# adaLN products moved to TensorE strips, low parts moved from GpSimd, and the RG-LRU output norm folded into the projection, in a transformer block on one core

## The chip, the core and the metric

The kernel runs on one core of one Trainium2 chip. The core has TensorE (PE, matrix products; its weight loads are listed as PEld), VectorE (DVE), ScalarE (ACT), GpSimd (POOL), and SyncE (SP), whose queue starts nearly all DMAs. The metric is the device time of one execution in microseconds, the median of several runs; lower is better.

## The reference, cut to what matters

One block of width 1024 over 2048 rows, all in fp32. `c` conditions both norms through a product with a 1024 x 6144 matrix (adaLN):

```
c_act = silu(c)
sh1, sc1, g1, sh2, sc2, g2 = split(c_act @ ada_w + ada_b, 6)
h = rmsnorm(x, mix_norm_g) * (1 + sc1) + sh1
z = h @ w_in                       # 1024 x 2328, split into q, keys, values, gates, zx, zy
o_nsa = three-branch sparse attention(q, keys, values, gates)
o_lru = RG-LRU scan(conv(zx)) * gelu(zy)
mixed = concat(rmsnorm(o_nsa, nsa_out_norm_g), rmsnorm(o_lru, lru_out_norm_g))
x = x + g1 * (mixed @ w_out)
h = rmsnorm(x, ffn_norm_g) * (1 + sc2) + sh2
x = x + g2 * conv_ffn(h)
return rmsnorm(x, final_norm_g)
```

## The kernel before

Every large product is made of fp32r pieces: an operand is split into a high part `h` (a copy rounded to fp32r, by ACT) and a low part `l` (the rest, by a subtraction), and `mm3` sums the three products hh, hl and lh. So each weight tile and each input tile costs an ACT copy and a subtraction before PE can use all of it. The order of the instructions on every engine is set when the program is built, by a scheduler that plays a time line; on the chip each engine takes its own instructions in that order.

The program has three phases. Phase 1 makes the in-projection in four chunks of 512 rows; phase 2 makes the attention and the output projection in 16 tiles of 128 rows; phase 3 makes the feed forward in four chunks.

Phase 1 starts with the modulation of the first norm. `ada_pair(k)` makes the shift and the scale of the features of block k (two blocks of 128 columns of the adaLN matrix, 512 KB each, loaded to `adp`). It does so in one of three ways by the letter in `HOW`: D and M multiply the eight row tiles by `c_act` and add them up on DVE (`aa`, lines 225 and 227; for M half of it on ACT and POOL, lines 230 and 233), and P uses eight products on PE with one column of `c_act` as the weights (`apr`, line 215). A product with ones then sums `aa` over the partitions (`ap`, line 234), and DVE adds the bias (`mod`, line 235). The other 32 blocks of the matrix are made by `ada_block`, one after each in-projection tile (`ada_next`), always on DVE: one multiplication (line 168) and seven multiply-adds (line 170) into `aa`, then a product with ones (`ap`, lines 173 and 182). Their 512 KB inputs `ad` share the five buffers of the tag `x`.

Each chunk needs its rows normalised and transposed. `norm_x` loads four tiles of rows, ACT squares and scales them (lines 140 and 142); `norm_k` then makes one feature block of `hT`: four transposes on PE (`tp`, line 149), `hh` on ACT (line 153), `hf` on DVE (line 154), `hl` on POOL (line 155). Eight such blocks make the chunk's input.

Then PE makes the tiles of the chunk in this order: `zc` (two), `zx` (four, RG-LRU input), `zy` (four, its gate), `zq` (four), `zk` (two), `zv` (four, values and gates); the first four tiles of the first chunk are called `zf`. The weights of a tile are loaded to `wr` (512 KB), and their high and low parts are `w..h` (ACT, line 120) and `w..l` (POOL, line 121), three tiles deep. Between them the RG-LRU runs: convolution `xc` on DVE, its parts `xs`, the gate products `pg`, decay, scan (line 380), and `yy`, whose squares are summed to `sqs` (POOL, line 388). `lru_norm` sums `sqs` over the partitions with one fp32 product of 512 columns (`pr`, line 392), takes the square root and the reciprocal of it (`rb`, lines 394 and 395), multiplies `yy` by it (line 397) and stores high and low parts `ls` (POOL, line 401). In chunks 1 to 3 `wo_next` also scales rows of `w_out` (`wos`, DVE, line 316) from two loads, `g1b` and `wor`.

After the last chunk's value tiles come the compressed keys and values (`ph`, with inputs `xbh` and `xbl`), and phase 2 begins with the first score product `sa`.

Of the kernel before, what the change touches and what calls it, by code (L numbers as in the profile page):

```python
# [50 lines left out]
def hymba_block(ctx, tc, x, vecs, rows, ada, w_in, w_v, lru_w, cmp_w1, cmp_w2, w_out, w_gu, w_dn,  # L51
# [9 lines left out]
    # scratch in DRAM: what one phase hands to the next  # L61
# [10 lines left out]
    # ---------------------------------------------------------------- constants  # L72
# [19 lines left out]
    epsb = cst.tile([P, 1], F32, name="epsb")  # L92
    pool.memset(epsb, EPS)
# [7 lines left out]
    gates = cst.tile([P, NQ, 24], F32, name="gates")  # L101
    VC = cst.tile([P, G, P], F32R, name="VC")
# [14 lines left out]
    def split(pl, raw, shape, name, tag, bufs, lo_eng=None):  # L117
# [28 lines left out]
    def norm_k(pl, pp, xs, c, k, Acol, Bcol, hbufs):  # L146
# [52 lines left out]
    with tc.tile_pool(name="a", bufs=1, reuse_waits="tile") as pl, tc.tile_pool(name="ap", bufs=1, space=PSUM, reuse_waits="tile") as pp:  # L199
# [377 lines left out]
        while adaq:  # L577
            ada_next()
# [462 lines left out]
```

## Time and profile before

| | us |
|---|---|
| median of the three runs | 3023.27 |
| lowest and highest of them | 3020.88, 3027.9 |
| profiled execution: span from its first to its last instruction | 3027.4 |
| TensorE busy in that span | 2853.5 (94%) |
| VectorE, ScalarE, GpSimd busy | 1872.6, 1457.8, 1662.2 |
| phase 1, up to the first score product | about 657 |

The profile gives the profiled execution as its span alone; that is 4.1 us (0.14%) above the median of the runs. All times inside the program are counted from the span's start. A product's busy time runs to its modelled end and overlaps the next one, so the pace of products is read from the distance of their starts.

### The profile page before, as it was taken

The numbers are of one execution on the slowest core, as the hardware profiler recorded it, in microseconds if no ns is written. First come the engines' busy times: TensorE is split into PE (matmuls) and PEld (weight loads), VectorE is DVE, ScalarE is ACT, GpSimd is POOL, SyncE is SP. The second block draws the span as 40 slices with busy tenths as digits, with TensorE's granted clock in tenths as the row PEclk, the third lists the DMA queues.
The fourth block names the chain that finished last, engine by engine and source line by source line (L and its number), as shares of the span: only waits on it lengthen the run. The fifth ranks groups of instructions, "written<-read, shape, count | busy, mean of one in ns | idle before, by whom it ended". The sixth has DMA issues, their size and how long they took to land. (4 is left out here: it accounts for less than half of the span.)

```text
span 3027.4 us, 39397 instructions
## 1 busy us (share of the span) xinstructions
PE 2853.5 (94%) x13676; PEld 2344.7 (77%) x13676; DVE 1872.6 (62%) x3373; ACT 1457.8 (48%) x2619; POOL 1662.2 (55%) x1584
## 2 busy tenths in 40 slices
PE   6989888968999999999999999999999999999998
PEld 4767676756778887888778888788887888888886
DVE  7778888775777888888756650466405663056620
ACT  4636353556677777777743332433325333233322
POOL 4555646557666566555534464644546445464444
PEclk8989899978999999999999999999999999999999
DMA  6465646555444433344253332433324333243332
GB/s 241 151 205 170 221 154 229 158 172 173 134 134 123 121 107 117 107 120 125 74 191 98 96 124 94 140 97 98 128 88 146 98 97 128 82 139 97 96 100 84
DMA packets 233064, 397.84 MB, mean 131 GB/s; under 512 B 20385, under 2 KB 143265, under 8 KB 232609
## 3 DMA queue, kind: packets, MB, share of 16 engines
q1 hardware_dynamic: 232256, 394.13, 41.0%
q8 instruction: 109, 1.79, 0.2%
q0 software_dynamic: 320, 1.05, 0.1%
q14 instruction: 91, 0.74, 0.1%
q10 hardware_dynamic: 288, 0.13, 0.0%
HBM read 342.16 MB, written 53.08 MB: 131 GB/s over the span
## 5 line engine op out<-in xcount | busy, mean ns | idle before, releaser
L906 DVE TENSOR_SCALAR ac<-gp,vec 128x512 f32<-128x512 f32 x88 | 189.2, 2150 | 215.3 <-ACT gp L903 208.2
L750 DVE TENSOR_TENSOR tl<-pt,th 128x512 fp32r<-128x512 f32 (+4 forms) x444 | 295.6, 684 | 40.8 <-ACT th L749 37.2
L749 ACT ACTIVATE th<-pt 128x512 fp32r<-128x512 f32 (+4 forms) x444 | 254.6, 593 | 111.8 <-PE pt L748 106.7
L938 DVE TENSOR_TENSOR o<-pt,o 128x128 f32<-128x128 f32 x128 | 28.3, 283 | 435.8 <-PE pt L935 435.8
L720 POOL TENSOR_SCALAR ps<-ps,rs,gates 128x1024 f32<-128x1024 f32 (+7 forms) x192 | 181.4, 956 | 146.3 <-DVE rs L717 93.1
L914 DVE TENSOR_TENSOR gl<-ac,gh 128x512 fp32r<-128x512 f32 x88 | 212.2, 2411 | 68.9 <-ACT gh L913 68.9
L909 ACT ACTIVATE ac<-ac 128x512 f32<-128x512 f32 x88 | 55.7, 632 | 316.2 <-DVE ac L908 316.2
L714 ACT ACTIVATE ps<-ps,mn 128x1024 f32<-128x1024 f32 (+7 forms) x192 | 171.1, 895 | 35.6 <-DVE mn L614 35.3
L748 PE MATMUL pt<-ident,ps 128*128 128x128 f32 x1088 | 168.4, 275 | 5.3 <-DVE tl L750 4.4
L121 POOL TENSOR_TENSOR wd_0l<-wd,wd_0h 128x1408 fp32r<-128x1408 f32 x32 | 103.1, 3223 | 126.1 <-ACT wd_0h L120 126.1
L609 PE MATMUL ss<-ks,Q 128*128 128x512 f32 (+3 forms) x640 | 165.3, 382 | 4.7 <-DVE mn L614 2.1
L748 PEld LDWEIGHTS pt<-ident,ps 128*128 128x128 f32 x1088 | 134.1, 141 | 41.6 <-DVE tl L750 10.8
L121 POOL TENSOR_TENSOR wd_1l<-wd,wd_1h 128x1408 fp32r<-128x1408 f32 x32 | 103.2, 3224 | 110.6 <-ACT wd_1h L120 110.6
L908 DVE SCALAR_TENSOR_TENSOR ac<-gp,vec,ac 128x512 f32<-128x512 f32 x176 | 137.9, 783 | 6.1
L609 PEld LDWEIGHTS ss<-ks,Q 128*128 128x128 f32 x640 | 117.0, 196 | 31.6 <-DVE mn L614 6.4
L128 PE MATMUL pd<-gl,wd_0h 128*128 128x512 f32 x352 | 139.8, 397 | 0.0
L128 PE MATMUL pd<-gh,wd_0h 128*128 128x512 f32 x352 | 137.7, 391 | 0.0
L128 PE MATMUL pd<-gl,wd_1h 128*128 128x512 f32 x352 | 137.6, 391 | 0.0
L128 PE MATMUL pd<-gh,wd_0l 128*128 128x512 f32 x352 | 137.5, 391 | 0.0
L128 PE MATMUL pd<-gh,wd_1l 128*128 128x512 f32 x352 | 137.5, 390 | 0.0
L128 PE MATMUL pd<-gh,wd_1h 128*128 128x512 f32 x352 | 137.4, 390 | 0.0
L760 PE MATMUL po<-tl,vs 128*128 128x512 f32 x272 | 123.4, 454 | 2.0 <-DVE tl L750 2.0
(1564 smaller groups left out, 9053.4 us busy)
## 6 DMA issues: line engine op xcount, KB each, us to landing
wg<-in_w_gu_dram SPq DMA_DIRECT2D x88, 512.0 KB, 3.5
wu<-in_w_gu_dram SPq DMA_DIRECT2D x88, 512.0 KB, 3.5
wd<-in_w_dn_dram SPq DMA_DIRECT2D x64, 704.0 KB, 4.0
wr<-in_w_in_dram SPq DMA_DIRECT2D x64, 512.0 KB, 4.3
ad<-in_ada_dram SPq DMA_DIRECT2D x32, 512.0 KB, 5.4
Q<-Q_d SPq DMA_DIRECT2D x64, 256.0 KB, 4.0
ks<-K_d SPq DMA_DIRECT2D x56, 256.0 KB, 3.5
vs<-V_d SPq DMA_DIRECT2D x56, 256.0 KB, 3.0
```

The costliest lines, as they stand in the source:

```text
L121: (lo_eng or pool).tensor_tensor(l, raw, h.bitcast(F32), op=OP.subtract)
L128: pe.matmul(ps, a, b, start=(n == 0), stop=(n == total - 1))
L609: pe.matmul(ps[:, o:o + W], Qt[:, hl, h * P:(h + 1) * P], K_ap, start=(hl == 0), stop=(hl == 1))
L714: act.activation(p, p, AF.Exp, scale=-1.0, bias=init, accum_out=sm[:, h, 2 + n:3 + n])
L720: pool.tensor_scalar(p, p, rs[:, h, 2:3], gt[:, h, 1:2], op0=OP.mult, op1=OP.mult)
L748: pe.transpose(pt[:, h * P:(h + 1) * P], jobs[n][0](h), ident)
L749: act.activation(th, pt, AF.Copy)
L750: dve.tensor_tensor(tl, pt, th.bitcast(F32), op=OP.subtract)
L760: pe.matmul(po, jobs[n][1], tl, start=False, stop=(n == N - 1))
L906: dve.tensor_scalar(ac, gp[:, 0:TC], V("fcw", f), V("fcb", f), op0=OP.mult, op1=OP.add)
L908: dve.scalar_tensor_tensor(ac, gp[:, k:k + TC], V("fcw", k * NF + f), ac, op0=OP.mult, op1=OP.add)
L914: dve.tensor_tensor(l, ac, h.bitcast(F32), op=OP.subtract)
```

## The change

1. **adaLN on PE.** `caz` holds `c_act` as eight weight tiles of 32 columns, of which 31 are zero. `ada_product` multiplies a block's eight row tiles by them with eight fp32 products of 128 columns; row tile q writes the 32 partitions from 32 (q mod 4) on, so the first four start four strips of one PSUM tile and the other four add to them. ACT copies the strips to SBUF (`adr`), and a product with ones sums them over the partitions (`ada_columns`, line 179, or line 192 for the gate of the residual), one step later than the product for the 32 later blocks. All eight pairs and all 32 blocks go this way; `aa` and `HOW` are gone. The later blocks load into one buffer of their own (`ad`), and the tag `x` has four buffers instead of five.
2. **Low parts.** In phase 1 `split` subtracts on DVE: weights, `xs`, `ls`. Phase 3's weights stay on POOL (`wload`). `sqs` is summed on DVE.
3. **Norm.** `hl` no longer comes from POOL: DVE makes `hf` as ps * A - hh, and ACT adds the bias and rounds. This holds for phase 1 and for the three later chunks of phase 3.
4. **RG-LRU output norm.** `lru_out` stores `yy` without the norm, and 16 products of one column give the row sums; their inverse root `rlru` is the scale of ACT's copy of the projection's first half in phase 2.

Cut to what the text speaks of, comments aside:

```diff
-        (lo_eng or pool).tensor_tensor(l, raw, h.bitcast(F32), op=OP.subtract)
+        (lo_eng or dve).tensor_tensor(l, raw, h.bitcast(F32), op=OP.subtract)
...
-        dve.tensor_scalar(f, ps, Acol[:, k:k + 1], Bcol[:, k:k + 1], op0=OP.mult, op1=OP.add)
-        pool.tensor_tensor(l, f, h.bitcast(F32), op=OP.subtract)
+        dve.scalar_tensor_tensor(f, ps, Acol[:, k:k + 1], h.bitcast(F32), op0=OP.mult, op1=OP.subtract)
+        act.activation(l, f, AF.Identity, bias=Bcol[:, k:k + 1])
...
+    def ada_product(pl, pp, caz, raws, name):
+        n = len(raws)
+        ps = pp.tile([P, n * P], F32, name=f"apr{name}", tag="g", bufs=2)
+        for j, raw in enumerate(raws):
+            for q in range(KT):
+                o = 32 * (q % 4)
+                pe.matmul(ps[o:o + 32, j * P:(j + 1) * P], caz[:, q, :], raw[:, q, :], start=(q < 4), stop=(q >= 4))
+        r = pl.tile([P, n * P], F32, name=f"adr{name}", tag="adr", bufs=2)
+        act.activation(r, ps, AF.Copy)
+        return r
+    def ada_columns(pp, r, b, n, step, name):
+        p1 = pp.tile([P, n], F32, name=f"ap{name}", tag="g", bufs=2)
+        for j in range(n):
+            pe.matmul(p1[:, j:j + 1], r[:, j * P:(j + 1) * P], ones[:, 0:1], start=True, stop=True)
+        cols = slice(b, b + (n - 1) * step + 1, step)
+        o = VEC["ada_b"][0] + b
+        dve.tensor_tensor(mod[:, cols], p1, vec[:, o:o + (n - 1) * step + 1:step], op=OP.add)
+    def ada_steps(pl, pp, caz, b):
+        raw = pl.tile([P, KT, P], F32, name=f"ad{b}", tag="ad", bufs=1)
         sync.dma_start(raw, ada[b])
-        acc = pl.tile([P, P], F32, name=f"aa{b}", tag="adacc", bufs=2)
-        dve.tensor_scalar(acc, raw[:, 0, :], cact[:, 0:1], None, op0=OP.mult)
-        for k in range(1, KT):
-            dve.scalar_tensor_tensor(acc, raw[:, k, :], cact[:, k:k + 1], acc, op0=OP.mult, op1=OP.add)
+        r = ada_product(pl, pp, caz, [raw], f"b{b}")
...
-            pe.matmul(ps, ones, acc, start=True, stop=True)
+            pe.matmul(ps, ones, r, start=True, stop=True)
...
-            ps = pp.tile([P, 1], F32, name=f"ap{b}", tag="g", bufs=2)
-            pe.matmul(ps, acc, ones[:, 0:1], start=True, stop=True)
-            dve.tensor_tensor(mod[:, b:b + 1], ps, V("ada_b", b), op=OP.add)
+            ada_columns(pp, r, b, 1, 1, f"c{b}")
+        yield
...
-                ("junk", 2048, 1), ("ii", 8192, 1), ("th", 8192, 1), ("yy", 8192, 1), ("x", 4096, 5), ("t2", 2048, 2),
+                ("ii", 8192, 1), ("th", 8192, 1), ("yy", 8192, 1), ("x", 4096, 4), ("ad", 4096, 1), ("t2", 2048, 2),
...
+        caz = pl.tile([P, KT, 32], F32, name="caz")
+        dve.memset(caz, 0.0)
+        dve.tensor_copy(caz[:, :, 0:1], cact.unsqueeze(2))
...
-            if how == 'P':
-                ps = pp.tile([1, 2 * P], F32, name=f"apr{k}", tag="g", bufs=2)
-                for q in range(KT):
-                    pe.matmul(ps, cact[:, q:q + 1], raw[:, :, q, :], start=(q == 0), stop=(q == KT - 1))
-                r = pl.tile([1, 2 * P], F32, name=f"adr{k}", tag="ge", bufs=2)
-                act.activation(r, ps, AF.Copy)
-            for j in range(2):
-                p1 = pp.tile([P, 1], F32, name=f"ap{k}_{j}", tag="g", bufs=2)
-                if how == 'P':
-                    pe.matmul(p1, r[:, j * P:(j + 1) * P], ones[0:1, 0:1], start=True, stop=True)
-                else:
-                    acc = pl.tile([P, P], F32, name=f"aa{k}_{j}", tag="adacc", bufs=2)
-                    if j == 0 or how == 'D':
-                        dve.tensor_scalar(acc, raw[:, j, 0, :], cact[:, 0:1], None, op0=OP.mult)
-                        for q in range(1, KT):
-                            dve.scalar_tensor_tensor(acc, raw[:, j, q, :], cact[:, q:q + 1], acc, op0=OP.mult, op1=OP.add)
-                    else:
-                        for q in range(KT):
-                            act.activation(raw[:, j, q, :], raw[:, j, q, :], AF.Copy, scale=cact[:, q:q + 1])
-                        for w in (4, 2, 1):
-                            dst = raw[:, j, 0:w, :] if w > 1 else acc.unsqueeze(1)
-                            pool.tensor_tensor(dst, raw[:, j, 0:w, :], raw[:, j, w:2 * w, :], op=OP.add)
-                    pe.matmul(p1, acc, ones[:, 0:1], start=True, stop=True)
-                dve.tensor_tensor(mod[:, 8 * j + k:8 * j + k + 1], p1, V("ada_b", 8 * j + k), op=OP.add)
+            r = ada_product(pl, pp, caz, [raw[:, 0], raw[:, 1]], f"p{k}")
+            ada_columns(pp, r, k, 2, 8, f"p{k}")
...
-        ada_pair(0, "xc", HOW[0])
-        xs0 = norm_x(pl, x, 0, 5)
+        ada_pair(0, "xc")
+        xs0 = norm_x(pl, x, 0, 4, ("t2", 2))
...
+        adap = []
         def ada_next():
+            new = None
             if adaq:
-                ada_block(pl, pp, adaq.pop(0), "x", 5)
+                new = ada_steps(pl, pp, caz, adaq.pop(0))
+                next(new)
+            if adap:
+                next(adap.pop())
+            if new:
+                adap.append(new)
 
...
-                    pool.tensor_tensor(sqs, sqs, t2, op=OP.add)
-
-            def lru_norm():
-                pr = pp.tile([P, TC], F32, name=f"pr{c}", tag="g", bufs=2)
-                pe.matmul(pr, ones, sqs, start=True, stop=True)
-                rb = pl.tile([P, TC], F32, name=f"rb{c}", tag="sqs", bufs=1)
-                act.activation(rb, pr, AF.Sqrt, scale=1.0 / 512.0, bias=epsb)
-                dve.reciprocal(rb, rb)
+            def lru_out():
                 for m in range(4):
-                    dve.tensor_tensor(yy[:, m], yy[:, m], rb, op=OP.mult)
                     if c + 1 < NCH:
                         st = pl.tile([P, 2, TC], F32R, name=f"ls{c}_{m}", tag="st", bufs=3)
                         act.activation(st[:, 0], yy[:, m], AF.Copy)
-                        pool.tensor_tensor(st[:, 1], yy[:, m], st[:, 0].bitcast(F32), op=OP.subtract)
+                        dve.tensor_tensor(st[:, 1], yy[:, m], st[:, 0].bitcast(F32), op=OP.subtract)
                         sync.dma_start(L_d[:, :, m, t0:t0 + TC], st.bitcast(F32))
                     else:
                         for n, t in enumerate(split(pl, yy[:, m], [P, TC], f"ls{c}_{m}", "h", 12)):
                             sync.dma_start(L_d[:, n, m, t0:t0 + TC], t.bitcast(F32))
-
-            # --- attention inputs
+                pr = pp.tile([P, 4], F32, name=f"pr{c}", tag="g", bufs=2)
+                for t in range(4):
+                    pe.matmul(pr[:, t:t + 1], sqs[:, t * P:(t + 1) * P], ones[:, 0:1], start=True, stop=True)
+                rl = rlru[:, 4 * c:4 * c + 4]
+                dve.tensor_scalar(rl, pr, 1.0 / 512.0, EPS, op0=OP.mult, op1=OP.add)
+                pool.tensor_tensor(rl, rl, nhalf, op=OP.pow)
...
-                act.activation(t, p1, AF.Copy)
+                act.activation(t, p1, AF.Copy, scale=rlru[:, i:i + 1])
...
-            return split(pl, raw, [P, n, P], name, "w", 2, lo_eng)
+            return split(pl, raw, [P, n, P], name, "w", 2, lo_eng or pool)
```

What moves on TensorE in the first chunk's first key tile (`zk`, 24 products): before, the sum of the adaLN block `aa` stands behind the tile's sixth product.

```order
L128 MATMUL zk_0_1293<-hh_1_225,w14h 128x512
L128 MATMUL zk_0_1293<-hl_1_226,w14h 128x512
L128 MATMUL zk_0_1293<-hh_1_225,w14l 128x512
L173 MATMUL ap_1063<-aa_1054,ones 128x128 [waits DVE_49]
L128 MATMUL zk_0_1293<-hh_2_270,w14h 128x512
```

After, the same place holds the strips of one block (`aprb`, eight products) and the sum of the block before it (`ap` from `adrb`).

```order
L128 MATMUL zk_0_1302<-hh_0_191,w14h 128x512 [waits DVE_49,Activation_49]
L128 MATMUL zk_0_1302<-hl_0_192,w14h 128x512
L170 MATMUL aprb_959<-ad_957,caz 32x128 [waits DMAHW0_49,DVE_49]
L170 MATMUL aprb_959<-ad_957,caz 32x128 x7
L192 MATMUL ap_970<-adrb_917,ones 128x128 [waits Activation_49]
L128 MATMUL zk_0_1302<-hh_0_191,w14l 128x512
```

The product that waited for DVE's eight `aa` instructions is gone; in its place PE waits for the load of `ad`, and for ACT, which made `adrb`.

What moves on VectorE at the start of chunk 1, behind the last feature blocks of the norm: before, adaLN sums, then one scaling of `w_out`, then the convolution.

```order
L170 SCALAR_TENSOR_TENSOR aa_1853<-ad_1851,cact,aa_1853 128x128 [waits DVE_49]
L170 SCALAR_TENSOR_TENSOR aa_1920<-ad_1918,cact,aa_1920 128x128 [waits DVE_49]
L170 SCALAR_TENSOR_TENSOR aa_1853<-ad_1851,cact,aa_1853 128x128 [waits DVE_49]
L170 SCALAR_TENSOR_TENSOR aa_1920<-ad_1918,cact,aa_1920 128x128 [waits DVE_49] x4
L316 SCALAR_TENSOR_TENSOR wos_2105<-wor_2103,vec,g1b_2101 128x1024 [waits DMAHW5_49,DMAHW7_49,DMAHW4_49,DMAHW3_49]
L350 TENSOR_SCALAR xc_1736<-xp_0_1772,vec 128x512 [waits Activation_49,Pool_49]
```

After, the last two `hf`, an adaLN bias, both scalings of that chunk, and then the low parts of the weights of `zx` tiles 1 to 3, which were POOL's before.

```order
L154 SCALAR_TENSOR_TENSOR hf_6_1500<-tp_6_1493,A_79,hh_6_1498 128x512 [waits DVE_49,Activation_49]
L154 SCALAR_TENSOR_TENSOR hf_7_1511<-tp_7_1504,A_79,hh_7_1509 128x512 [waits DVE_49,Activation_49]
L182 TENSOR_TENSOR mod<-apc_1811,vec 128x1 [waits PE_49]
L324 SCALAR_TENSOR_TENSOR wos_2131<-wor_2129,vec,g1b_2127 128x1024 [waits DMAHW7_49,DMAHW2_49,DMAHW0_49]
L324 SCALAR_TENSOR_TENSOR wos_2234<-wor_2232,vec,g1b_2230 128x1024 [waits DMAHW6_49,DMAHW2_49,DMAHW1_49]
L121 TENSOR_TENSOR w21l<-wr_1716,w21h 128x1024 [waits PE_49,Activation_49]
L121 TENSOR_TENSOR w22l<-wr_1755,w22h 128x1024 [waits PE_49,Activation_49]
L121 TENSOR_TENSOR w23l<-wr_1814,w23h 128x1024 [waits DMAHW5_49,PE_49,Activation_49]
```

The low parts w21l, w22l and w23l now stand behind two instructions that wait for loads.

What moves on SP's queue between the chunks: before, the load of an adaLN block stands among the stores of keys and values and waits for DVE to free one of five buffers.

```order
L424 DMA K_d<-ks_0_1318 64x2x512 [waits DVE_49]
L424 DMA K_d<-ks_0_1318 64x2x512 [waits DMAHW7_49]
L166 DMA ad_1654<-in_ada_dram 128x1024 [waits DMAHW0_49,DVE_49]
L424 DMA K_d<-ks_1_1354 64x2x512 [waits DMAHW1_49,DVE_49]
L424 DMA K_d<-ks_1_1354 64x2x512 [waits DMAHW2_49]
L439 DMA V_d<-vs_0_1545 128x2x256 [waits DMAHW3_49,DVE_49]
```

After, it waits for PE to finish the block before it, which stands in the same single buffer, and the load of the weights of a `zx` tile (`wr`) is behind it.

```order
L405 DMA L_d<-ls_3_1380 256x1x512 [waits DMAHW7_49,DVE_49]
L448 DMA V_d<-vs_2_1612 128x2x256 [waits DMAHW0_49,DVE_49]
L187 DMA ad_1666<-in_ada_dram 128x1024 [waits PE_49]
L267 DMA wr_1755<-in_w_in_dram 128x1024 [waits DMAHW2_49,DVE_49]
L448 DMA V_d<-vs_3_1642 128x2x256 [waits DMAHW3_49,DVE_49]
```

The load can only start once the product before it on PE is done, and whatever waits in front of it on SP delays it too.

## Rows read from the trace of the kernel before

**Rows 1.** The page: busy time of each engine, its share, its instructions.
```profile
PE 2853.5 (94%) x13676; PEld 2344.7 (77%) x13676; DVE 1872.6 (62%) x3373; ACT 1457.8 (48%) x2619; POOL 1662.2 (55%) x1584
```

**Rows 2.** Busy time by stretches: length, engines in turn, granted clock, DMA share, GB/s.
```profile
0.00:657.00 657.00, 544.09 (x2484) 440.10 (x2484) 528.02 (x791) 315.02 (x456) 361.58 (x270) 0.92 0.57 187
657.00:3027.00 2370.00, 2309.42 (x11192) 1904.57 (x11192) 1344.58 (x2582) 1142.78 (x2163) 1300.57 (x1314) 0.99 0.37 116
...
140.00:220.00 80.00, 61.12 (x282) 49.58 (x281) 62.92 (x95) 33.12 (x47) 44.35 (x30) 0.87 0.61 199
220.00:300.00 80.00, 75.61 (x329) 60.22 (x329) 64.30 (x102) 49.79 (x68) 45.78 (x34) 1.00 0.52 176
```

**Rows 3.** TensorE's waits, 0 to 657 us: total us, times, longest.
```profile
PE ap L182 <- DVE aa L170: 15.4, 5, 4.7
...
PE ph L128 <- DVE xbl L494: 9.1, 4, 3.5
...
PE ap L173 <- DVE aa L170: 8.1, 2, 5.0
PE pr L392 <- POOL sqs L388: 7.9, 3, 4.7
PE ap L234 <- DVE aa L227: 6.0, 2, 4.2
PE pg L128 <- DVE mod L183: 5.1, 3, 3.1
PE zv L128 <- POOL w35l L121: 5.0, 1, 5.0
PE ap L182 <- DVE mod L183: 4.6, 2, 3.3
PE ap L234 <- DVE mod L235: 4.1, 1, 4.1
...
PE ap L234 <- POOL aa L233: 3.9, 1, 3.9
...
PE zv L128 <- POOL w17l L121: 1.2, 1, 1.2
```

**Rows 4.** TensorE in order of time, 140 to 165 us: start, length, instruction, idle before.
```profile
144.40 0.39 PE L128 MATMUL zk<-hh,w14h 128*128 128x512 f32 x1
144.63 0.40 PE L128 MATMUL zk<-hl,w14h 128*128 128x512 f32 x1
...
150.92 0.80 PE L173 MATMUL ap<-aa,ones 128*128 128x128 f32 x2 [4.96 <-DVE aa L170]
```

**Rows 5.** Instructions of tiles aa and w14l: shortest/median/longest ns, first and last start.
```profile
L170 DVE SCALAR_TENSOR_TENSOR aa<-ad,cact,aa x224: 253/352/2526, 70.0 to 497.6; 128x128 f32<-128x128 f32 x112
...
L121 POOL TENSOR_TENSOR w14l<-wr,w14h x1: 2408/2408/2408, 140.6 to 140.6; 128x1024 fp32r<-128x1024 f32 x1
```

**Rows 6.** Instructions of the tile wo in phase 2, same columns.
```profile
L598 DVE TENSOR_TENSOR wo<-wr,wo x8: 1192/1225/1574, 670.3 to 690.2; 128x1024 fp32r<-128x1024 f32 x8
```

**Rows 7.** Busy time of the apr products alone, at 1.2 and 2.4 GHz.
```profile
59.50:61.50 2.00, 2.00 (x5) 0.57 (x6) 0.00 (x0) 0.50 0.00 0
61.50:64.00 2.50, 2.50 (x12) 0.84 (x10) 0.00 (x0) 1.00 0.00 0
```

**Rows 8.** DMA issues, 0 to 657 us: count, KB each, median us to landing.
```profile
ad<-in_ada_dram SPq DMA_DIRECT2D x32, 512.0 KB, 5.4
...
wor<-in_w_out_dram SPq DMA_DIRECT2D x8, 512.0 KB, 6.5
```

**Rows 9.** VectorE's waits, 0 to 657 us: total us, times, longest.
```profile
DVE wos L316 <- DMA wor<-in_w_out_dram: 26.5, 7, 6.7
```

**Rows 10.** Instructions of the tile wos: shortest/median/longest ns.
```profile
L316 DVE SCALAR_TENSOR_TENSOR wos<-wor,vec,g1b x8: 1279/1702/2478, 222.8 to 512.5; 128x1024 f32<-128x1024 f32 x8
```

**Rows 11.** Costliest groups by shape, 0 to 657 us: busy, mean ns, idle before.
```profile
L155 POOL TENSOR_TENSOR hl<-hf,hh 128x512 fp32r<-128x512 f32 x32 | 42.2, 1333 | 46.0 <-DVE hf L154 44.9 <-DMA adp<-in_ada_dram 0.9
...
L153 ACT ACTIVATE hh<-tp,mod,A 128x512 fp32r<-128x512 f32 x32 | 24.4, 773 | 56.7 <-PE tp L149 23.6 <-DVE A L236 23.0 <-PE ap L234 6.7
```

More of the change, by code (lines that the diff above doesn't have):

```diff
@@ L91, in hymba_block @@
     pool.memset(nhalf, -0.5)
-    epsb = cst.tile([P, 1], F32, name="epsb")
-    pool.memset(epsb, EPS)
     mod = cst.tile([P, 48], F32, name="mod")
@@ L101, in hymba_block @@
     gates = cst.tile([P, NQ, 24], F32, name="gates")
+    rlru = cst.tile([P, NQ], F32, name="rlru")
     VC = cst.tile([P, G, P], F32R, name="VC")
@@ L130, in mm3, with norm_x @@
         return n
-    def norm_x(pl, src, c, xbufs):
+    def norm_x(pl, src, c, xbufs, jt=("junk", 1)):
         xs = []
@@ L137, in norm_x @@
             sync.dma_start(xt, src[c * TC + t * P:c * TC + (t + 1) * P, :])
-            junk = pl.tile([P, D], mybir.dt.bfloat16, name=f"j{c}_{t}", tag="junk", bufs=1)
+            junk = pl.tile([P, D], mybir.dt.bfloat16, name=f"j{c}_{t}", tag=jt[0], bufs=jt[1])
             ss = pl.tile([P, 1], F32, name=f"ss{c}_{t}", tag="ss", bufs=4)
@@ L309, in wo_next @@
             k = woq.pop(0)
-            g1b = pl.tile([P, D], F32, name=f"g1b{k}", tag="x", bufs=5)
+            g1b = pl.tile([P, D], F32, name=f"g1b{k}", tag="x", bufs=4)
             sync.dma_start(g1b, G1_d)
-            raw = pl.tile([P, D], F32, name=f"wor{k}", tag="x", bufs=5)
+            raw = pl.tile([P, D], F32, name=f"wor{k}", tag="x", bufs=4)
             sync.dma_start(raw, w_out[k])
@@ L387, in chunk @@
                     act.activation(t2, yy[:, m], AF.Square)
-                    pool.tensor_tensor(sqs, sqs, t2, op=OP.add)
-            def lru_norm():
-                pr = pp.tile([P, TC], F32, name=f"pr{c}", tag="g", bufs=2)
-                pe.matmul(pr, ones, sqs, start=True, stop=True)
-                rb = pl.tile([P, TC], F32, name=f"rb{c}", tag="sqs", bufs=1)
-                act.activation(rb, pr, AF.Sqrt, scale=1.0 / 512.0, bias=epsb)
-                dve.reciprocal(rb, rb)
+                    dve.tensor_tensor(sqs, sqs, t2, op=OP.add)
+            def lru_out():
                 for m in range(4):
-                    dve.tensor_tensor(yy[:, m], yy[:, m], rb, op=OP.mult)
                     if c + 1 < NCH:
@@ L447, in chunk @@
                 zs(range(8, 14))
-                lru_norm()
-                nxt = norm_T(pl, pp, x, c + 1, A1, B1, 5, 12)
+                lru_out()
+                nxt = norm_T(pl, pp, x, c + 1, A1, B1, 4, 12, jt=("t2", 2))
                 v_tiles()
@@ L454, in chunk @@
                 zs(PRE)
-                lru_norm()
+                lru_out()
                 v_tiles()
@@ L479, in compress_step @@
             wh, wl = weights(NCH - 1, "c", q)
-            xh = pl.tile([P, 4, G, P], F32R, name=f"xbh{q}", tag="x", bufs=5)
-            xl = pl.tile([P, 4, G, P], F32R, name=f"xbl{q}", tag="x", bufs=5)
+            xh = pl.tile([P, 4, G, P], F32R, name=f"xbh{q}", tag="x", bufs=4)
+            xl = pl.tile([P, 4, G, P], F32R, name=f"xbl{q}", tag="x", bufs=4)
             o = VEC["pos"][0] + 16 * n + 4 * qd
@@ L532, in hymba_block @@
             if k:
-                ada_pair(k, ("xc", "rr", "ii")[k % 3], HOW[k])
+                ada_pair(k, ("xc", "rr", "ii")[k % 3])
             hT.append(norm_k(pl, pp, xs0, 0, k, A1, B1, 12))
@@ L576, in hymba_block @@
             hT = chunk(c, hT)
-        while adaq:
+        while adaq or adap:
             ada_next()
```

12 lines of the change are left out of this document (5 added, 7 removed).

## The prediction

> **What bounds the kernel now.** I read the page first: TensorE is busy for 94% of the span [rows 1]. The average hides two different parts, so next come the stretches [rows 2]. From 657 us on, PE is busy for 2309 of 2370 us at a granted clock of 0.99: there PE is the bound, and apart from the norm's `hf` and `hl`, off PE's chain, and the scale inside an existing ACT copy, the change puts nothing into it. In the first 657 us (phase 1) PE is busy for 544 us only, so it idles 113 us, and the mean clock is 0.92. The clock has two levels, 1.2 and 2.4 GHz; a mean of 0.92 over 657 us is 2 x 0.08 x 657 = 105 us at the lower one. The two go together: the stretch 140 to 220 us, around the change of chunk, has 61 us of PE work in 80 us and a clock of 0.87; the next 80 us have 76 us at 1.00 [rows 2]. DVE is busy for 528 of the 657 us, the most after PE.
>
> What PE waits for stands in the third view [rows 3]. The reader should group it by what the change touches. Sums of adaLN on DVE and POOL (`aa`): 15.4 + 8.1 + 6.0 + 3.9 = 33.4 us. The bias additions of the same blocks, late in DVE's queue (`mod`): 5.1 + 4.6 + 4.1 = 13.8 us. The square sum of the RG-LRU on POOL: 7.9 us. Low parts of value weights on POOL, four rows from 5.0 down to 1.2, I take them as 13 us in all. Together 68 us. The other 45 us are the start, the compressed keys (`xbl`, 9.1) and small waits. One such wait in time order: the key tile runs at 0.23 us a product, then PE stops for 4.96 us behind the product that waits for `aa` [rows 4].
>
> Why DVE is late is seen in the spread of one instruction: `aa` takes 352 ns at the median, up to 2526 [rows 5]. The longest is about the length of POOL's subtraction on a weight tile, 2408 ns [rows 5], so now and then DVE stands still for one of POOL's. With these subtractions on DVE, POOL has next to nothing left in phase 1.
>
> **The change part by part.**
>
> *Removed.* The four groups above, 68 us. Their share of the lost clock: PE works in about two thirds of the 105 us at 1.2 GHz (estimate), so the clock costs about half of 70, 35 us; I give the removed waits their share, 35 x 68 / 113 = 21 us. Sum -89 us. Bounds: at least the waits for `aa` alone, -33; at most all idle time and clock, -148.
>
> *DVE's new work.* 80 low parts of weights (eighteen tiles in each of four chunks, eight more for the compressed keys and values) at 1.2 us, the same instruction shape as in phase 2 [rows 6], make 98 us. Against it, 287 multiply-adds and 41 first multiplications of `aa` go, 224 of which alone have a median of 352 ns [rows 5], and the two parts of the norm of `yy`. DVE does no more than now, and without POOL's blocks. I cost this at nothing: it lies under PE's 544 us of work. If that cover is gone, a low part is 1.2 us late per weight tile.
>
> *TensorE's strips.* 48 blocks x 8 = 384 fp32 products of 128 columns. The trace has no strips. The nearest row is `apr`, fp32 with one weight column and 256 moving columns: sixteen records (eight products, two passes each) in 4.5 us, 2.0 of them at 1.2 GHz and 2.5 at 2.4 [rows 7]. With x us a pass at 2.4 GHz, 2.0/2x + 2.5/x = 16 gives x = 0.22, so 0.44 us a product of 256 columns and 0.22 us one of 128. All 384 in a row: 84 us. If four strips ran side by side: 21 us. I take a value between: the two passes of one product go to the same strip, one behind the other, and only the second can run beside the first pass of the next strip's product. That makes 9 pass lengths for 16, 84 x 9/16 = 47 us. Gone are 16 products of `apr`, 7 us. Net +40; bounds +14 and +77.
>
> Here a page speaks. The Trainium skill, "TensorEngine Tiling (Array Packing)", Key Properties, says that tiles in different columns of the array are independent and may load and multiply in parallel, up to four times as fast where the weights have at most 32 columns. By it the strips would cost the 21 us. The same section says that a change of the tiling mode drains the array, and each block changes it twice; no run here shows that cost.
>
> *New waits.* In chunks 1 to 3 DVE's low parts stand behind two scalings of `w_out`, each waiting for loads. DVE waits for them today too, 26.5 us in seven times, up to 6.7 [rows 9], but no low part is behind it. After the change: the loads start when the last transposes have freed their buffers and land after 6.5 us [rows 8], perhaps 8 for the second pair; two scalings at 1.28 [rows 10] and the first low part at 1.2 follow, so it is ready 10.3 to 11.8 us after the transposes. PE has 39 products in front of the one that needs it, 39 x 0.23 = 9 us. That is 1.3 to 2.8 us, three times: +6 us (bounds 0 and 20, three times 6.7).
>
> The single buffer `ad`: a load lands after 5.4 us [rows 8] and may start only when the product before it is done. Within a chunk 30 products or more lie between two blocks, 7 us, and hide it. Where chunks meet, about seven lie between (1.6 us): 3.8 us, three times; half of it falls into the time that PE waits for the norm anyway: +6 us (bounds 0 and 16). Behind that load on SP is the weight tile of a `zx`, two tiles ahead of its use.
>
> *Norm and RG-LRU.* `hl` leaves POOL, 1.33 us each, one behind the other; on ACT it adds to `hh` at 0.77 [rows 11], about 1.4 to 1.5 us a block if it costs no more than that one. PE uses a block for three tiles, nine products, 2.1 us: hidden. The 16 one-column products replace four fp32 ones of 512 columns, a gain under 3 us that I leave out. In phases 2 and 3 the cost is nothing, under PE's 2309 us.
>
> *Sum.* -89 + 40 + 6 + 6 = -37 us. The span of the profiled execution is 4.1 us above the median of the runs; the difference is set against the median: 3023.3 - 37 = 2986 us.
>
> **The rivals.**
>
> A. Strips side by side, four at a time (the page's rule). For it: different partitions of the output; against it: two passes to the same strip follow each other. +14 in place of +40: 2960 us.
>
> B. Strips one after another, as `apr` ran. For it: the only fp32 row does so. +77: the sum is 0, and the change does not shorten the span: 3023 us, a little less if the longer products fill other waits.
>
> C. ACT takes DVE's place where chunks meet. For it: ACT gets 32 `hl` and 40 copies of `adr`; against it: 315 of 657 us [rows 2]. A backlog of 6 us at three changes of chunk: +18, 3004 us.
>
> D. Slower: each of the 32 later blocks holds PE until its load lands. For it: the load waits for PE and stands in one in-order queue with stores that wait for DVE; against it: landing in 5.4 us against 7 us of other products. It decides from 37/32 = 1.2 us a block on; at 3 us a block, +96 - 6 for what I have counted: 3076 us.
>
> **How the numbers follow.** Forecast 0.37, A 0.27, B 0.16, C 0.12, D 0.08. The likeliest gives 2986 us. The range of the forecast alone is 2970 to 3006, by the upper bounds of the new waits (+24) and some of A. To hold 8 in 10 it takes in A, with a few us of removed waits more, C and half of B: 2940 to 3020. Within 0.2% (6 us), about what a measurement of this kernel can tell from no change, I put half of B; the rest of B lies half on each side. Faster: 0.37 + 0.27 + 0.12 + 0.04 = 0.80; same 0.08; slower 0.08 + 0.04 = 0.12.
>
> **What would show it.** Right: no wait for `aa`, `sqs` or a POOL low part; PE idle under 60 us before the first `sa`, which comes at about 620; the longest DVE instructions of phase 1 near their medians; POOL under 80 us there. The strips: busy time of `aprb` and `aprp` near 47 us, or 21 (A), or 84 (B). D shows as waits of `aprb` for the load of `ad`; the `w_out` step as waits of `zx` for w21l and its fellows in later chunks; C as waits of `zc` for `hl`. From `sa` on all should read as before. The prediction is wrong if PE's idle time in phase 1 stays near 113 us with other names, or if phase 2 or 3 moves.

## The result and the profile after

The changed kernel takes 2944.86 us (median of 4 runs, 2943.12 to 2946.36) against 3022.07 before (the median of four runs; the table above had three): 0.9743 of the time, 95% interval 0.973 to 0.9755, or 77 us less. The forecast was 37 us less. The profiled execution has a span of 2943.8 us, 83.6 less than the one before.

The page's busy times after the change, in the order of [rows 1]: PE rises from 94 to 97% of the span.

```profile
PE 2848.2 (97%) x14436; PEld 2341.0 (80%) x14436; DVE 1698.5 (58%) x3149; ACT 1499.2 (51%) x2686; POOL 1324.8 (45%) x1396
```

The first `sa` comes at 576.8 us (657.0 before). Busy time in the two parts, columns as in [rows 2]:

```profile
0.00:576.80 576.80, 539.61 (x3245) 436.72 (x3245) 359.06 (x567) 338.84 (x500) 58.37 (x108) 0.98 0.65 214
576.80:2943.80 2367.00, 2308.61 (x11192) 1904.28 (x11192) 1339.45 (x2582) 1160.32 (x2187) 1266.45 (x1288) 0.99 0.39 116
```

Phase 1 carries 80.2 of the 83.6 us, the rest 3.4 (2370.4 to 2367.0). PE's idle time in phase 1 falls from 657.0 - 544.1 = 112.9 us to 37.2, and the granted clock rises from 0.92 to 0.98: 2 x 0.02 x 577 = 23 us at the lower level in place of 105. DVE is busy for 359 us where it was 528, GpSimd for 58 where it was 362. What PE still waits for before the first `sa` answers to [rows 3]:

```profile
PE aprp L170 <- DVE lamt L568: 6.1, 1, 6.1
PE zc L128 <- ACT hh L153: 5.7, 2, 4.4
PE tp L149 <- ACT x L142: 3.5, 2, 2.1
PE ph L128 <- DVE xbl L503: 3.2, 3, 1.2
PE ph L128 <- DVE qs L421: 2.7, 1, 2.7
...
PE aprb L170 <- DMA ad<-in_ada_dram: 1.8, 1, 1.8
...
PE zv L128 <- DVE w69l L121: 1.4, 1, 1.4
...
PE zc L128 <- ACT hl L155: 0.4, 1, 0.4
...
PE tp L149 <- DVE hf L154: 0.3, 1, 0.3
```

The waits for `aa`, `mod`, `sqs` and GpSimd's low parts are gone. The first row is the start: it names `lamt`, which happened to end then, but the first product needs the load of `adp`; the profile of e3, below, puts the same wait (6.1 us) down to that load. The second row is new. The last had 8.2 us before, in the same view of the kernel before:

```profile
PE tp L149 <- DVE hf L154: 8.2, 7, 3.2
```

Next, PE's products of the adaLN sums and of the RG-LRU norm in phase 1, by shape: busy time, mean ns of one | idle before them. First the kernel before, then the changed one.

```profile
L215 PE MATMUL apr<-adp,cact 128*1 128x256 f32 x32 | 9.3, 455 | 0.0
L182 PE MATMUL ap<-ones,aa 128*128 128x1 f32 x48 | 7.7, 236 | 21.0 <-DVE aa L170 15.4 <-DVE mod L183 4.6 <-ACT rr L339 0.9
...
L392 PE MATMUL pr<-sqs,ones 128*128 128x512 f32 x8 | 5.5, 769 | 10.0 <-POOL sqs L388 7.9 <-POOL xf L490 2.1
...
L234 PE MATMUL ap<-ones,aa 128*128 128x1 f32 x24 | 4.8, 275 | 23.2 <-DVE lamt L558 9.2 <-DVE aa L227 6.0 <-DVE mod L235 4.1
...
L173 PE MATMUL ap<-aa,ones 128*128 128x128 f32 x16 | 3.9, 329 | 8.1 <-DVE aa L170 8.1
```

```profile
L170 PE MATMUL aprb<-ad,caz 128*32 128x128 f32 x512 | 22.2, 283 | 1.8 <-DMA ad<-in_ada_dram 1.8
L170 PE MATMUL aprp<-adp,caz 128*32 128x128 f32 x256 | 12.3, 330 | 6.2 <-DVE lamt L568 6.1 <-DMA adp<-in_ada_dram 0.2
L179 PE MATMUL apc<-ones,adrb 128*128 128x1 f32 x48 | 9.3, 263 | 0.0
L179 PE MATMUL app<-ones,adrp 128*128 128x1 f32 x32 | 5.0, 260 | 1.1 <-ACT adrp L172 1.1
...
L192 PE MATMUL ap<-adrb,ones 128*128 128x128 f32 x16 | 3.9, 326 | 0.0
L411 PE MATMUL pr<-ones,sqs 128*128 128x1 f32 x32 | 3.8, 240 | 0.0
```

These products took 31.2 us before and take 56.5 now, 25.3 more; the strips alone are 34.5. All other products of phase 1 took 544.1 - 31.2 = 512.9 us and take 539.6 - 56.5 = 483.1: the same instructions in 29.8 us less, at the higher clock. So the whole account is: idle -75.7, products of the sums +25.3, other products -29.8, later phases -3.4, together -83.6.

Last, how long one instruction of DVE takes, shortest, median and longest ns: the multiply-adds of the convolution `xc`, which the change doesn't touch, before and after.

```profile
L352 DVE SCALAR_TENSOR_TENSOR xc<-xp,vec,xc x48: 739/752/2944, 86.0 to 535.5; 128x512 f32<-128x512 f32 x48
```

```profile
L360 DVE SCALAR_TENSOR_TENSOR xc<-xp,vec,xc x48: 743/748/753, 61.8 to 460.5; 128x512 f32<-128x512 f32 x48
```

The median is the same. Before, some took 2.2 us longer, about as long as one of GpSimd's weight subtractions [rows 5]; now none does.

The same holds for all of VectorE's instructions of phase 1, each set against the quicker quarter of its own kind. Before, 119 of 791 are more than 0.4 us longer than that, 169 us together of the 528, and every one of them overlaps an instruction of GpSimd; after the change there is none. A single case: a sum `aa` that begins at 141.65 us takes 1.51 us and ends 0.15 us after the subtraction `w14l` [rows 5], which ran when it began. The text calls such an instruction stopped.

### The profile page after: what moved, and what is told of

Read it like the earlier page. It is cut to its first block, busy times and chain, and to the rows that moved or that the text cites. A ratio compares the mean times of both kernels' runs of the same rounds, so it can differ in the third digit from the quotient of the medians.

```text
span 2943.8 us, 40502 instructions
## 1 busy us (share of the span) xinstructions
PE 2848.2 (97%) x14436; PEld 2341.0 (80%) x14436; DVE 1698.5 (58%) x3149; ACT 1499.2 (51%) x2686; POOL 1324.8 (45%) x1396
## 6 DMA issues: line engine op xcount, KB each, us to landing
wg<-in_w_gu_dram SPq DMA_DIRECT2D x88, 512.0 KB, 3.6
wu<-in_w_gu_dram SPq DMA_DIRECT2D x88, 512.0 KB, 3.6
wr<-in_w_in_dram SPq DMA_DIRECT2D x64, 512.0 KB, 4.4
ad<-in_ada_dram SPq DMA_DIRECT2D x32, 512.0 KB, 4.8
```

## The experiments

The theory that the prediction left behind: VectorE was late because GpSimd's long subtractions stop it, so that nearly all the idle time and the low clock of phase 1 hang on those, not on the named waits alone. The rival: the strips take the late sums out of PE's way, and that is the gain. One part was undone at a time, then parts were made alone. The kernel before was run again beside each group of kernels (medians 3021.35 to 3024.62 us), and differences to it are taken against those runs. The profiles, with the changed kernel for comparison:

| kernel | median us | ratio to before, interval | first `sa` | PE busy, idle ahead of it | clock |
|---|---|---|---|---|---|
| before | 3022.07 | | 657.0 | 544.1, 112.9 | 0.92 |
| all parts | 2944.86 | 0.973 to 0.9755 | 576.8 | 539.6, 37.2 | 0.98 |
| e1, low parts on GpSimd | 2971.93 | 0.9821 to 0.9859 | 601.3 | 545.5, 55.8 | 0.97 |
| e2, sums on VectorE | 2930.66 | 0.9683 to 0.972 | 564.3 | 515.6, 48.7 | 0.97 |
| e3, one strip | 2992.59 | 0.9886 to 0.9923 | 623.4 | 595.6, 27.8 | 0.99 |
| e4, old RG-LRU norm | 2933.13 | 0.9691 to 0.9725 | 568.6 | 533.4, 35.2 | 0.98 |
| e5, `hl` on GpSimd | 2943.47 | 0.9719 to 0.9756 | 578.6 | 542.8, 35.8 | 0.98 |
| e6, own buffers for `ls` | 2955.18 | 0.9759 to 0.9795 | 583.0 | 542.3, 40.7 | 0.97 |
| e7, strips alone | 2996.06 | 0.9893 to 0.9935 | 622.9 | 551.0, 71.9 | 0.96 |
| e8, low parts alone | 2953.92 | 0.9745 to 0.9788 | 587.2 | 523.2, 64.0 | 0.96 |
| e9, low parts and `hl` | 2929.17 | 0.9674 to 0.9703 | 565.5 | 516.1, 49.4 | 0.97 |
| e10, strips at the start | 2920.45 | 0.9649 to 0.9678 | 556.5 | 513.7, 42.8 | 0.98 |
| e11, e10 with the old norm | 2930.97 | 0.9683 to 0.9713 | 562.9 | 515.4, 47.5 | 0.97 |
| e12, e10 with row scaling on VectorE | 2911.57 | 0.9612 to 0.9641 | 545.3 | 512.0, 33.3 | 0.98 |

**e1, the low parts back on GpSimd.**

```diff
-        (lo_eng or dve).tensor_tensor(l, raw, h.bitcast(F32), op=OP.subtract)
+        (lo_eng or pool).tensor_tensor(l, raw, h.bitcast(F32), op=OP.subtract)
...
```

> The changed kernel (2945 us) with the low parts of phase 1's split tiles back on GpSimd; strips, `hl` on ACT and the row scale stay. Theory 1, the waits and the low clock of phase 1 come from GpSimd and VectorE holding each other up, and each part of the change frees a share: the GpSimd low parts are waited for again (13 us before), VectorE's longest instructions grow to 2 us or more, the time rises by 15 to 35 us, to 2960 to 2980. Theory 2, nearly the whole gain lies in the low parts leaving GpSimd: 50 us or more, 2995 to 3020. Theory 3, the strips carry the gain and the engine of the low parts is beside the point: within 6 us of 2945.

27 us slower than all parts. The instruction from above, and two of PE's waits:

```profile
L360 DVE SCALAR_TENSOR_TENSOR xc<-xp,vec,xc x48: 740/752/2945, 64.5 to 478.2; 128x512 f32<-128x512 f32 x48
```

```profile
PE pg L128 <- DVE mod L182: 6.8, 2, 3.6
...
PE ph L128 <- DVE xbl L503: 5.6, 4, 2.2
```

VectorE's longest are back at 2.9 us, though it has no sums to do: 66 of its instructions are stopped, for 102 us. The time lies in theory 1's range.

**e2, the sums back on VectorE, ACT and GpSimd**, with the loads in five buffers of `x` as before.

```diff
-        r = ada_product(pl, pp, caz, [raw], f"b{b}")
...
+        dve.tensor_scalar(acc, raw[:, 0, :], cact[:, 0:1], None, op0=OP.mult)
+        for k in range(1, KT):
+            dve.scalar_tensor_tensor(acc, raw[:, k, :], cact[:, k:k + 1], acc, op0=OP.mult, op1=OP.add)
...
```

> The changed kernel with the adaLN sums back where they were (VectorE, ACT and GpSimd, the two `apr` pairs on PE), loads in five buffers of x; low parts on VectorE, `hl` on ACT and the row scale stay. The strips (about 42 us of PE by the changed kernel's trace) are gone. Theory 1: VectorE now has low parts and sums (about 480 of 580 us), so waits for `aa` and `mod` of 30 to 50 us come back and with them some low clock: 2950 to 2980. Theory 2, VectorE was late only because of GpSimd: its `aa` stay at 352 ns, PE waits for them under 10 us, and without the strips the time falls below the changed kernel's, to 2905 to 2930. Theory 3, the strips carry the gain: 3000 or more.

14 us faster than with strips, 0.7 us above theory 2's range and with its signs. VectorE's sums, and PE's longest waits:

```profile
L169 DVE SCALAR_TENSOR_TENSOR aa<-ad,cact,aa x224: 325/348/355, 56.9 to 422.5; 128x128 f32<-128x128 f32 x112
```

```profile
PE ap L233 <- DVE lamt L558: 9.2, 1, 9.2
PE zc L128 <- ACT hh L153: 8.8, 3, 3.8
...
PE ap L233 <- POOL aa L232: 3.9, 1, 3.9
...
PE ap L233 <- DVE aa L226: 1.1, 1, 1.1
```

The same `aa` that took up to 2526 ns [rows 5] takes at most 355. PE waits 1.3 us for VectorE's sums in all of phase 1 (the row of 1.1 and one of 0.2), where it was 15.4 + 8.1 + 6.0, and not at all for `mod`; the 3.9 us for a sum on GpSimd stay. VectorE is busy for 446 of 564 us with sums and low parts, and on time. So these waits go without the strips; e8, below, shows that the subtractions leaving GpSimd are enough.

**e3, one strip.**

```diff
-                o = 32 * (q % 4)
-                pe.matmul(ps[o:o + 32, j * P:(j + 1) * P], caz[:, q, :], raw[:, q, :], start=(q < 4), stop=(q >= 4))
+                pe.matmul(ps[0:32, j * P:(j + 1) * P], caz[:, q, :], raw[:, q, :], start=(q == 0), stop=(q == KT - 1))
...
```

> The changed kernel with all eight adaLN products of a block written to one strip, rows 0 to 31, one accumulation; the column product reads 32 rows. Same count of products, same shape. If products to different strips overlap and that is why a pass takes 55 ns in the changed kernel, a pass to one strip takes about 107 ns as in `apr`, the strips cost about 84 in place of 42 us and the time rises by about 40 us, to 2985. If the 55 ns have nothing to do with strips (a 32-column product of 128 columns takes that long anyway): within 4 us of 2945.

48 us slower, more than the 40 that were expected. PE in order of time around one block, with four strips and then with one:

```profile
78.49 0.40 PE L128 MATMUL zy<-hh,w7h 128*128 128x512 f32 x1
78.82 0.64 PE L170 MATMUL aprb<-ad,caz 128*32 128x128 f32 x16
79.39 0.49 PE L192 MATMUL ap<-adrb,ones 128*128 128x128 f32 x2
```

```profile
94.43 0.40 PE L128 MATMUL zy<-hh,w7h 128*128 128x512 f32 x1
94.76 1.94 PE L169 MATMUL aprb<-ad,caz 128*32 128x128 f32 x16
96.62 0.48 PE L191 MATMUL ap<-adrb,ones 32*128 32x128 f32 x2
```

From start to start a block of eight products takes 0.57 us on four strips and 1.86 on one, 0.23 a product where the prediction had 0.22 from [rows 7]: by this pace strips run 3.3 side by side, not 16/9. By busy time, which holds the tail of each block, it is 96.4 us against 34.5, or 2.8 times; the 42 us of the expectations were too much. PE is busy 56 us more in phase 1, of which 9 take the place of idle time.

**e4, the RG-LRU norm as before**: square sum on GpSimd, product with ones, reciprocal and four multiplications.

```diff
+                act.activation(rb, pr, AF.Sqrt, scale=1.0 / 512.0, bias=epsb)
+                dve.reciprocal(rb, rb)
...
+                    dve.tensor_tensor(yy[:, m], yy[:, m], rb, op=OP.mult)
...
-                rl = rlru[:, 4 * c:4 * c + 4]
-                dve.tensor_scalar(rl, pr, 1.0 / 512.0, EPS, op0=OP.mult, op1=OP.add)
-                pool.tensor_tensor(rl, rl, nhalf, op=OP.pow)
...
```

> The changed kernel with the RG-LRU output norm as before (square sum on GpSimd, product with a matrix of ones, square root, reciprocal, four multiplications), its low parts on VectorE. As the prediction has it, the row scale gives back the wait for `sqs` (7.9 us) with its clock: 5 to 15 us slower than the changed kernel, 2950 to 2960. If GpSimd without its low parts is no longer late: within 3 us of 2945.

12 us faster, which neither theory had. PE waits 0.6 us for `sqs` on GpSimd, not 7.9: that wait too was GpSimd's other work. Where chunks meet, the two kernels wait for different things (the changed kernel 5.7 us for `hh`, above):

```profile
PE aprb L170 <- DMA ad<-in_ada_dram: 8.0, 4, 4.0
...
PE zc L128 <- ACT hh L153: 0.7, 1, 0.7
PE pr L400 <- POOL sqs L396: 0.6, 1, 0.6
```

These waits do not make the 12 us: PE's idle time differs by 2.0 us. Its products take 6.2 us less in phase 1, and the later phases 3.0 less (2364.0 after 2367.0); the granted clock of the whole run is 0.990 in place of 0.986. Why it is higher stays open.

**e5, `hf` and `hl` as before.**

```diff
-        dve.scalar_tensor_tensor(f, ps, Acol[:, k:k + 1], h.bitcast(F32), op0=OP.mult, op1=OP.subtract)
-        act.activation(l, f, AF.Identity, bias=Bcol[:, k:k + 1])
+        dve.tensor_scalar(f, ps, Acol[:, k:k + 1], Bcol[:, k:k + 1], op0=OP.mult, op1=OP.add)
+        pool.tensor_tensor(l, f, h.bitcast(F32), op=OP.subtract)
```

> The changed kernel with the norm's `hf` and `hl` as before (scale and shift on VectorE, `hl` as a subtraction on GpSimd); all else as changed. The prediction costed this edit at nothing. Theory 1, GpSimd is now nearly idle, so `hl` there is neither late nor long enough to hold VectorE up: within 6 us of 2945. Theory 2, ACT is the engine that is late where chunks meet, and 32 `hl` taken off it help: 2930 to 2939. Theory 3, every 512-column subtraction on GpSimd stops VectorE, as the weights' low parts did: 2951 to 2960.

No difference (2943.47), as theory 1 has it. None of VectorE's instructions is stopped, although `hl` is on GpSimd.

**e6, buffers of their own for `ls`**, a guess at the 12 us of e4: `ls` is ready earlier without the norm, and in ACT's queue it waits, ahead of `hh`, for the stores of `ks`.

```diff
+                tags = ("xsh", "xsl") if m < 2 else ("ge", "ge")
+                h, l = [pl.tile([P, TC], F32R, name=f"ls{c}_{m}{n}", tag=tg, bufs=2) for n, tg in zip("hl", tags)]
...
-                    if c + 1 < NCH:
+                    if c + 1 < NCH and m < 3:
...
```

> The changed kernel; only the split of the RG-LRU output (`ls`) of chunks 0 to 2 gets buffers of its own for three of four pieces (free ones of `xsh`, `xsl`, `ge`), so that it no longer waits for the stores of `ks` out of the three `st` buffers. Theory 1, the row scale is slower than the norm it replaced (the run before: 12 us) because it makes `ls` ready earlier, and in ACT's queue they now stand ahead of the next chunk's `hh` and wait there for `st` (6.2 us in all): with own buffers the waits on `K_d` and `L_d` go and the time falls by 5 to 12 us, to 2933 to 2940. Theory 2, the cost lies in the 16 one-column products or in the later engines' order: within 3 us of 2945.

10 us slower, which neither theory had: the guess falls. The waits of `ls` are gone, but ACT stands behind other stores (4.3 us for `V_d` in the changed kernel), and `hh` is no earlier:

```profile
ACT vs L455 <- DMA V_d<-vs: 14.8, 5, 5.1
```

```profile
PE zc L128 <- ACT hh L153: 8.6, 3, 3.0
```

**e7, the strips alone, and e8, the low parts alone**, each put into the kernel before (in the main the diffs of e2 and e1, the other way round; e8 also moves `ls`). Both, and e9, keep one detail of the change: the squares of the rows (`j`) go to the two buffers `t2` in place of one of their own. No run has that detail alone.

> The kernel before with only the adaLN sums changed to strips (with their buffers); low parts and `hl` on GpSimd, RG-LRU norm as before. Theory 1, the sums on VectorE were late because of GpSimd, and each part frees a share: waits for `aa` and `mod` go (47 us and their clock), 32 us of strips come: 2985 to 3005. Theory 2, strips are no gain where GpSimd still holds VectorE up, because another VectorE result is late in their place: 3010 to 3030. Theory 3, strips are the main gain: under 2975.

> The kernel before with only the low parts of phase 1's split tiles moved from GpSimd to VectorE (weights, `xs`, `ls`); sums, `hl` on GpSimd and RG-LRU norm as before. Theory 1, GpSimd's long subtractions are what made VectorE late, and with them gone VectorE carries sums and low parts at their own pace: 80 us or more of gain, 2925 to 2945. Theory 2, all parts are needed, since VectorE has about 480 us of work in 580: 2955 to 2985. Theory 3, low parts on VectorE make it later still: 3015 or more.

29 and 71 us faster than before (3024.62 beside them). e7 fits its theory 1; e8, at 2953.92, falls between its theories 1 and 2. The strips alone leave VectorE's longest at 2928 ns, with 63 instructions stopped for 101 us, and PE with waits for VectorE under other names; `mod` is still late:

```profile
PE pg L128 <- DVE mod L182: 12.0, 3, 6.0
PE ph L128 <- ACT xbh L500: 10.6, 4, 5.8
PE aprb L170 <- DMA ad<-in_ada_dram: 8.6, 4, 3.5
PE tp L149 <- DVE hf L154: 6.7, 3, 3.1
```

With the low parts alone, 28 instructions are stopped for 24 us, and the longest `aa` falls to about the length of one `hl` of GpSimd, no longer that of a weight's low part:

```profile
L169 DVE SCALAR_TENSOR_TENSOR aa<-ad,cact,aa x224: 251/347/1405, 66.3 to 449.8; 128x128 f32<-128x128 f32 x112
...
L155 POOL TENSOR_TENSOR hl<-hf,hh x56: 1272/1294/3140, 25.9 to 2468.2; 128x512 fp32r<-128x512 f32 x56
```

**e9, low parts and `hl`**, with sums and norm as before.

> The kernel before with the low parts on VectorE and `hl` on ACT; adaLN sums and RG-LRU norm as before. Runs so far: low parts alone 2954; with `hl` and the row scale but without strips 2931; all parts 2945; all but the row scale 2933. Theory 1, GpSimd's remaining work (32 `hl` of 1.33 us) still holds VectorE up where VectorE also carries the sums, and the row scale is worth little: 2930 to 2940. Theory 2, the row scale is worth its 12 us or more where the sums are on VectorE, and costs only beside the strips: 2945 to 2955.

95 us faster than before and 16 faster than all parts, 0.8 us below theory 1's range. With the sums on VectorE, taking `hl` off GpSimd is worth 25 us (2954 to 2929), and 7 instructions are still stopped, for 7 us; beside the strips, where `hl` stops nothing, it was worth nothing (e5). The row scale adds nothing to it (e2, 2931). So the low parts and `hl` make more than the whole gain in time, but the theory's "nearly all the idle time" is not borne out: of 112.9 us of PE's idle time e8 takes away 49 and e9 64.

**e10, strips for the eight pairs of the start, VectorE's sums for the 32 later blocks; e11, the same with the old norm.**

```diff
-                new = ada_steps(pl, pp, caz, adaq.pop(0))
...
+                ada_block(pl, pp, adaq.pop(0), "x", 5)
...
```

> A mixture: strips for the eight pairs of the start, where every product waits for the modulation, and VectorE's sums for the 32 later blocks, where they lie under PE's work; low parts, `hl` and row scale as changed. If the strips cost what they take on PE and are of use only where VectorE is late: the start of the changed kernel (first `zy` at 68.7 us against 73.7 with all sums on VectorE) and the rest of the kernel without strips, 2931 - 5 = 2926. If the time is set by how the queues happen to interleave where chunks meet: anywhere from 2925 to 2945.

> The same mixture with the RG-LRU norm as before. If the row scale costs 12 us here as it did beside all strips: 2912 to 2920. If that cost came from ACT's queue where chunks meet and VectorE's reciprocal and multiplications now stand in front of the sums: 2926 to 2940.

With the loads of the later blocks in five buffers as in e2, e10 is 24 us faster than all parts and 10 faster than e2, below both of its ranges: strips pay at the start, where PE waits for the modulation, and cost later (PE is busy for 513.7 us in place of 539.6). With the old norm (e11) it is 10.5 us slower, the opposite sign of e4 and in its second range. Again less than half of that is PE's idle time (4.7 us more); PE's products take 1.7 us more in phase 1, and the later phases 5.4 (2367.1 after 2361.7).

**e12, e10 and the scaling of the next chunk's rows on VectorE**, a step that the change does not have.

```diff
-            act.activation(xt, xt, AF.Copy, scale=r)
+            if c > 0 and jt[0] == "t2":
+                dve.tensor_scalar(xt, xt, r, None, op0=OP.mult)
+            else:
+                act.activation(xt, xt, AF.Copy, scale=r)
```

> The mixture of strips at the start and VectorE's sums later (2920), with one thing more that the change does not have: where chunks meet, the scaling of the next chunk's rows by their norm (four instructions of 1.13 us on ACT) moves to VectorE. Theory 1, ACT is what is late where chunks meet (PE waits 9.4 us for `hh`, three times), so 4.5 us less in its queue there take most of that wait and its clock: 2908 to 2916. Theory 2, PE waits there for the chain through `ls` and its stores, or VectorE becomes late in ACT's place: within 4 us of 2920 or slower.

9 us faster again, as theory 1 has it, and the fastest of all: 2911.57 us, 0.9626 of the time before. PE's wait for `hh` in e10, and what is left of PE's waits for the norm's tiles in e12:

```profile
PE zc L128 <- ACT hh L153: 9.4, 3, 3.7
```

```profile
PE tp L152 <- DVE hf L157: 5.7, 3, 3.9
PE tp L152 <- ACT x L145: 3.5, 2, 2.1
```

PE's wait for `hh` in `zc` falls from 9.4 to 0.6 us, while the one for `hf`, which VectorE makes, rises from 2.6 to 5.7; PE's idle time falls by 9.5 us. So ACT's queue is what was late for `hh` where chunks meet.

## Why the prediction was right or wrong

The direction and the place were right: phase 1 gains, the later phases stay, GpSimd has 58 us there (under 80 as forecast), the listed waits go, PE's idle time is 37 us (under 60). The time also lies within the stated range, 2940 to 3020, but that is in part luck: the lower end was drawn for strips that run four at a time (26 us) and a few us of waits more, while measured, the strips gave 15 us more than was forecast, and waits and clock 28.5. The sum was 46.6 us short of the profiled spans' difference, and each of its terms erred to the same side:

| term | forecast | measured |
|---|---|---|
| PE's waits: removed 68, new 12 | -56 | -75.7 |
| low clock | -21 | -29.8 |
| strips less the old products | +40 | +25.3 |
| later phases | 0 | -3.4 |
| sum | -37 | -83.6 |

*Removed.* This step failed, in size and in cause. The prediction saw that VectorE stands still "now and then" for one of GpSimd's subtractions, and then took the four groups of [rows 3] that the edits name as what goes, 68 us, leaving the other 45. The stops were not occasional: 169 of VectorE's 528 us. (Not every late sum is a stop: ahead of the wait of [rows 4], VectorE stood idle for 3.29 us until a load of `ar` landed.) And a VectorE that is stopped for 2 us makes whatever is next late: `hf` (8.2 us of waits before, 0.3 after) and `xbl` (9.1 and 3.2) went too. Of the 47 us for `aa` and `mod`, which the prediction counted with the sums that move to PE, 5.2 are left in e2 with the sums where they were. The step on VectorE's new work, at nothing, was right (PE waits 3.2 us in all for the weights' low parts that moved there), and with it the strips had no wait left to remove after the start: parts alone give 71 (e8) and 29 us (e7), 95 (e9) with low parts and `hl`, and 77 all together.

*Clock.* The share of 105 us at the lower level was taken as 68/113; 82 of them went. The price of one, a third of a us, was about right: 29.8/82 = 0.36, from clocks of two digits. Over the runs the clock follows PE's idle time: 113 us of idle time go with 0.92, 64 to 72 with 0.96, 41 to 56 with 0.97 or 0.98, 28 to 37 with 0.98 or 0.99.

*Strips.* 34.5 us in place of 47, the second term that was mis-sized. The pass length (0.22 us a product in a row) was right; the choice of 16/9 between four strips and one was wrong. e3 shows 3.3, nearer to rival A's four. The Trainium skill, "TensorEngine Tiling (Array Packing)", Theoretical Speedup, has up to four times as fast for a dimension of at most 32, here the 32 columns of the weights: by their pace the runs come within a fifth of it. The drain that Key Properties of this page of the Trainium skill gives for a change of mode is not to be told apart here: the step from a 512-column product into a block takes 0.33 us where the pace is 0.23, with four strips and with one.

*New waits.* 12 us were counted. No `zx` product waits for a low part behind `wos`; the single buffer `ad` costs 1.8. Rival C has its wait in their place, PE for `hh` and `hl` where chunks meet, 6.1 us against the 18 it was priced at. e12 shows, in the mixture, that this wait is ACT's queue.

*Row scale.* Costed at nothing. Against the old norm it is 12 us slower beside all strips (e4), 1.5 slower without them (e9 to e2, intervals overlap), and 10.5 faster with strips at the start alone (e11 to e10). What gives it these signs stays open: PE's waits hold less than half of either difference, for the rest PE's products take a longer or shorter time, in phase 1 and behind it (granted clock of the whole run 0.986 and 0.990 for all parts and e4, 0.988 and 0.985 for e10 and e11), and the one mechanism that was tried (e6) fell.

*Later phases.* The 3.4 us are within what these phases vary by in the fourteen profiles, 2361.7 to 2371.6 us.

Rivals B and D did not occur: products to different strips overlap, and the load of `ad` holds PE once.

## What to carry to other kernels

Look at the longest against the median of an engine's instructions before you put a wait down to the engine's load: a spread of 352 to 2526 ns says that something else stops it, and then everything queued on it is late, not only what the waits name. Remove the blocker first, and price the other edits against that kernel: here two of four parts made 95 us, and the strips for the later blocks then only cost time on PE, for sums that VectorE made on time. An edit that removes no wait of its own, as the row scale here once GpSimd was free, moved the time by some 10 us of either sign: time such an edit in the company in which it will stand.

## What the runs showed of the hardware

Not expected: with VectorE and GpSimd both busy, the price fell on VectorE's whole queue. It was busy for 528 us in phase 1 before, and for 446 in e2, where it does more. The Trainium skill, "SBUF — State Buffer", section "SBUF: two separate sides", has the two share a pair of ports, which a VectorE instruction with two inputs in SBUF and a GpSimd instruction that reads SBUF hold in turn, each for its whole length while the other blocks. The rows agree: the longest `aa` of the later blocks takes 2526 ns where GpSimd subtracts weight tiles (2408 for `w14l`), 1405 in e8, where it subtracts `hl` (median 1294), and 355 in e2 with neither. Not every instruction of VectorE is stopped: `hf`, which reads PSUM, stays near its median in the kernel before, with `hl` and the low parts on GpSimd.

```profile
L154 DVE TENSOR_SCALAR hf<-tp,A,mod x32: 710/800/812, 26.0 to 492.0; 128x512 f32<-128x512 f32 x32
```

So PE's waits for `hf` before point to what stood ahead of it in VectorE's queue. And at the pace of 0.57 us for eight strip products, the strips of a whole block cost PE less than three products of 512 columns (0.23 each).
